# Turned operands in the mixer of a macaron decoder layer: rows of both blocks at once, p of two heads at once, k left as it lands

## The chip, the cores and the metric

One core of one Trainium2 chip runs the whole layer as one program. The metric is the device time of one execution in microseconds (us). Engines are named PE (TensorE matmul), PEld (its weight load), DVE (VectorE), ACT (ScalarE), POOL (GpSimd) and SP (SyncE, which here only issues DMAs).

## What is computed

256 tokens of width 2048 pass one decoder layer: a SwiGLU block, a token mixer of two branches, and a second SwiGLU block, each added to the scaled stream and normalised.

```python
h = layer_norm(ALPHA * h + 0.5 * swiglu(h, ffn1), ln1)          # d_ff 5632
c_q, c_kv, k_r, dq, dk, dv, gate_mla, gate_diff = split(h @ w_in)
q = rms_norm(c_q) @ w_uq                  # 8 heads of 128 + 64; the 64 are turned by rope
k_nope, v = rms_norm(c_kv) @ w_uk, rms_norm(c_kv) @ w_uv
o_mla  = softmax(q k^T, causal) v         # 8 heads
o_diff = (softmax(q1 k1^T + alibi) - lam * softmax(q2 k2^T + alibi)) dv   # 4 heads, rms-normed
y = sigmoid(gate_mla) * (o_mla @ w_branch_mla) + sigmoid(gate_diff) * (o_diff @ w_branch_diff)
h = layer_norm(ALPHA * h + y @ w_out, ln2)
h = layer_norm(ALPHA * h + 0.5 * swiglu(h, ffn2), ln3)
```

## The kernel before

All tokens stay on the chip as two row blocks b of 128 rows. Weights stream in from DRAM, 512 KB at a time. The large products keep fp32 accuracy with a split into a high and a low part: ACT casts a weight tile to the high part (L154), DVE takes the difference as the low part (L155), and three matmuls (hi x hi, hi x lo, lo x hi; lines L208, L209, L210) make one product. A unit of the schedule is one weight tile: its DMA, its cast and difference, and its matmuls, mostly 12.

**Order.** Each engine runs its own instructions in the order in which the program writes them. `unit` loads a tile, prepares it some units ahead of use in a ring of weight pairs (`wring`) and then writes its matmuls. `later(n, f)` writes f's instructions n units further on. So the side work of the mixer (softmaxes, transposed operands, gates) is strewn between the matmuls of the projections by the numbers given to `later`. `narrow_to(n)` sets how many pairs the ring has: six in the mixer. A pair takes two slots of the pool `act` (41 slots of 4 KB per partition). The pool `tmp` has six smaller slots, and products land in five PSUM banks (`mm`) and three (`tr`).

**Turning.** A matmul wants its activations with the model dimension on the partitions, so row blocks have to be transposed. Two ways are used. `rows_to_quad` transposes four 128x128 pieces with TensorE. `turn` goes through DRAM: DVE transposes a 128x512 row in squares of 32x32 into a tile "blocks" (`turn_out`, L715), POOL issues four writes of 64 KB (L717) into a DRAM tile "turn", some units later POOL issues the read of 256 KB into a tile "turned" (L729), and the user casts it (`turn_to_quad`, into the operands od, cn and y) or copies it into place (`turn_to_cols`, L737, for dqT, dkT, qT, qrT and kT). A quad is 512 of the model dimension. "blocks" and, for copies, "turned" lie in `tmp`. p of the softmax takes the same road in `turn_p`: one write "pturn" (L1107) and four reads "pt" (L1112).

**The mixer in time.** First come cn, ckv, the gates and the dq, dk, dv projections, then the four differential heads (scores L1237, values L1257 to L1259) between projections for the gates and for q, k and v of MLA; then the eight MLA heads (scores L1307 and L1309, values L1323 and L1324) between branch projections; then for f = 0 to 3 the product of om with the MLA branch, whose gated sum is y; then w_out on yq, whose quads f are turned as above. `v` is copied out of a bank at L1296, "junk" (L1263) is ACT's sum of squares of a differential head's output.

**h of the SwiGLU.** The product of gate and up is turned to DRAM (`hT`), and `get_h` (L895, POOL) reads a quad back as "hraw" when the down projection is near. The first three quads read are 3, 4 and 0, asked for 3, 6 and 9 units into the last group of gate and up; "sraw" and "raw" are weight tiles that SP loads meanwhile (L420, L457).

## Time and profile before

| | |
|---|---|
| median of 3 runs | 1989.48 us (1987.44 to 1990.28) |
| profiled execution | 1989.51 us, span 1987.7 us |
| granted TensorE clock | 0.995 of full speed |
| PE, DVE, ACT, POOL busy | 1956.0, 1782.5, 1239.5, 350.7 us |
| DMA | 494.61 MB, 249 GB/s |

Busy shares are averages over the whole span. A row of the waits view gives engine, line, the engine and line it waited for, the total, the count and the longest. A row of the stretches view gives the bounds, the length, the busy time of PE, PEld, DVE, ACT and POOL (with instruction counts), the granted clock, the busy share of the DMA engines and the GB/s. A row of the timeline gives start, duration, engine, line and operation, and in brackets the idle time ahead of it and what ended that. Groups give busy time and mean ns of one, then idle time before them. DMA rows give KB each and the median us from issue to landing.

### The profile page before, as it was taken

How to read it: one execution, taken by the hardware profiler on the slowest of the kernel's cores; microseconds unless marked ns; L12 is line 12 of the kernel's file. 1: busy time of each engine (PE TensorE's matmuls, PEld its weight loads, DVE VectorE, ACT ScalarE, POOL GpSimd, SP SyncE). 2: the span in 40 equal slices, each digit the busy share in tenths (PEclk: the TensorE clock that was granted, in tenths of full speed). 3: DMA queues.
4: the chain of work that ended last, by engine and by line, in shares of the span. 5: the costliest groups of instructions: out<-in, count | busy, mean ns of one | idle time of the engine just before them, and what ended most of it. 6: DMA issues, size and time to landing. Idle time of an engine off the chain costs nothing.

```text
span 1987.7 us, 25775 instructions
## 1 busy us (share of the span) xinstructions
PE 1956.0 (98%) x8716; PEld 1615.6 (81%) x8716; DVE 1782.5 (90%) x2191; ACT 1239.5 (62%) x1616; POOL 350.7 (18%) x603
## 2 busy tenths in 40 slices
PE   9999999999999999999998998999999999999997
PEld 7888888878888898888886786888888888788886
DVE  8999999998998879989986767789999999999986
ACT  6666666676665566666655654466666676665662
POOL 0112111222100010102246531001121112110000
PEclk9999999999999999999999999999999999999999
DMA  8978887878776666777677887779788878787763
GB/s 316 284 227 261 269 257 235 253 235 304 273 237 206 222 234 237 237 240 238 222 236 235 246 284 261 235 243 277 228 263 269 248 244 254 243 313 253 277 233 125
DMA packets 151444, 494.61 MB, mean 249 GB/s; under 512 B 22560, under 2 KB 22608, under 8 KB 151312
## 3 DMA queue, kind: packets, MB, share of 16 engines
q1 hardware_dynamic: 117360, 397.99, 58.1%
q0 software_dynamic: 33952, 94.98, 18.1%
q8 instruction: 68, 1.11, 0.2%
q14 instruction: 64, 0.52, 0.1%
HBM read 459.59 MB, written 33.29 MB: 248 GB/s over the span
## 4 chain that ended last, share of the span: by engine, by line
PE 86%; DMA 5%; DVE 4%; issue 2%; POOL 1%; ACT 1%; SPq 0%; DVEq 0%; POOLq 0%; ACTq 0%
PE mm L209 27%; PE mm L210 27%; PE mm L208 27%; DVE wring L155 2%; DMA turn<-blocks 1%; DMA turned<-turn 1%; DMA sraw<-in_gu_dram 1%; PE tr L209 1%; PE tr L210 1%; PE tr L208 1%; DVE sraw L428 1%; DMA pt<-pturn 1%; POOL turn L717 1%; ACT wring L154 1%; DMA gate<-gates 0%
## 5 line engine op out<-in xcount | busy, mean ns | idle before, releaser
L154 ACT CAST wring<-raw 128x1024 fp32r<-128x1024 f32 (+2 forms) x467 | 480.5, 1036 | 295.5 <-PE mm L210 196.4
L155 DVE TENSOR_TENSOR wring<-raw,wring 128x1024 fp32r<-128x1024 f32 (+2 forms) x467 | 556.9, 1202 | 85.4 <-ACT wring L154 83.6
L154 ACT CAST wring<-sraw 128x1024 fp32r<-128x1024 f32 x436 | 453.3, 1052 | 228.9 <-DVE sraw L428 95.0
L155 DVE TENSOR_TENSOR wring<-sraw,wring 128x1024 fp32r<-128x1024 f32 x436 | 521.2, 1222 | 19.4 <-ACT wring L154 16.5
L208 PE MATMUL mm<-wring,h 128*128 128x512 f32 (+2 forms) x1248 | 481.6, 386 | 2.3 <-ACT v L1296 2.3
L209 PE MATMUL mm<-wring,h 128*128 128x512 f32 (+2 forms) x1248 | 480.5, 385 | 0.2 <-DVE wring L155 0.2
L210 PE MATMUL mm<-wring,h 128*128 128x512 f32 (+2 forms) x1248 | 480.4, 385 | 0.0
L209 PE MATMUL mm<-wring,xs 128*128 128x512 f32 x776 | 302.3, 390 | 2.7 <-DVE wring L155 2.7
L208 PE MATMUL mm<-wring,xs 128*128 128x512 f32 x776 | 302.2, 389 | 0.0
L210 PE MATMUL mm<-wring,xs 128*128 128x512 f32 x776 | 302.0, 389 | 0.0
L208 PEld LDWEIGHTS mm<-wring,h 128*128 128x128 f32 x1248 | 234.7, 188 | 49.4 <-ACT v L1296 2.7
L209 PEld LDWEIGHTS mm<-wring,h 128*128 128x128 f32 x1248 | 234.8, 188 | 47.1 <-DVE wring L155 1.0
L210 PEld LDWEIGHTS mm<-wring,h 128*128 128x128 f32 x1248 | 234.8, 188 | 47.0 <-DVE h L155 0.7
L428 DVE TENSOR_TENSOR sraw<-sraw,sraw 128x1024 f32<-128x1024 f32 x168 | 199.4, 1221 | 3.7 <-DMA sraw<-in_wdv_dram 2.5
L209 PEld LDWEIGHTS mm<-wring,xs 128*128 128x128 f32 x776 | 145.7, 188 | 34.1 <-DVE wring L155 3.8
L208 PEld LDWEIGHTS mm<-wring,xs 128*128 128x128 f32 x776 | 145.6, 188 | 30.2
L210 PEld LDWEIGHTS mm<-wring,xs 128*128 128x128 f32 x776 | 145.7, 188 | 30.1
L717 POOL DMA_DIRECT2D hT<-blocks x176 | 96.9, 563 | 376.1 <-DVE blocks L715 373.7
L209 PE MATMUL mm<-wring,x 128*128 128x512 f32 x336 | 131.2, 390 | 1.0 <-DVE wring L155 0.9
L208 PE MATMUL mm<-wring,x 128*128 128x512 f32 x336 | 130.8, 390 | 0.0
L210 PE MATMUL mm<-wring,x 128*128 128x512 f32 x336 | 130.6, 389 | 0.0
L430 POOL DMA_DIRECT2D sraw<-in_gu_dram x40 | 35.4, 893 | 372.1 <-DVE sraw L428 368.9
(299 smaller groups left out, 2320.4 us busy)
## 6 DMA issues: line engine op xcount, KB each, us to landing
sraw<-in_gu_dram SPq DMA_DIRECT2D x160, 512.0 KB, 5.4
raw<-in_gu_dram SPq DMA_DIRECT2D x159, 512.0 KB, 4.9
raw<-in_dn_dram SPq DMA_DIRECT2D x140, 512.0 KB, 4.9
sraw<-in_gu_dram POOLq DMA_DIRECT2D x40, 512.0 KB, 7.1
sraw<-in_dn_dram SPq DMA_DIRECT2D x36, 512.0 KB, 5.9
hraw<-hT POOLq DMA_DIRECT2D x68, 256.0 KB, 6.5
eraw<-in_gu_dram SPq DMA_DIRECT2D x64, 256.0 KB, 5.8
raw<-in_w_out_dram SPq DMA_DIRECT2D x32, 512.0 KB, 5.2
```

The lines of the kernel that those rows point to most:

```text
L154: cast[0] = S.copy(hi, src)
L155: lows[0] = V.tensor_tensor(out=lo, in0=src, in1=hi.bitcast(F32), op=ALU.subtract)
L208: PE.matmul(o, xh, wh, start=first, stop=False, skip_group_check=again)
L209: PE.matmul(o, xh, wl, start=False, stop=False, skip_group_check=again)
L210: PE.matmul(o, xl, wh, start=False, stop=last, skip_group_check=again)
L428: last = V.tensor_tensor(out=R[src][i], in0=R[src][i], in1=R[add[1]][i], op=ALU.add)
L430: nc.gpsimd.dma_start(R["12"][s], source("22", s), accum_op=ALU.add)
L717: turned_out[0] = nc.gpsimd.dma_start(to.rearrange("(g r) (i f) -> i r g f", g=4, i=4)[i], t[32 * i:32 * (i + 1), :].rearrange("r (g f) -> ...
```

## The change

1. `turn_both` and `Cols`: the rows of both blocks share one "blocks" tile of 128x1024, four writes and one read of 512 KB. It serves qT, kT, qrT and the outputs of a pair of differential heads (od). dqT and dkT still leave row by row (`Cols.row`), but read back into one tile. All these tiles come from `act` rather than `tmp`.
2. k as the trip leaves it: dkT and kT are no longer copied into place; the score matmuls read them in runs of 32 columns (`keys`). Queries still are (`ordered`).
3. p of two MLA heads goes in one "pturn" of 128x768 and four reads "pt".
4. The ring has five pairs from the values projection of the differential heads to the end of the mixer, then six again.
5. y's last quad (f = 3) is transposed by TensorE (`rows_to_quad`); the last 512 rows of w_out are laid out to match. Quad 2's waits are (2, 3) units instead of (3, 3).
6. The first three quads of h are read by SP (`get_half`), one block at a time, at units 1, 3, 5, 7, 9 and 11.
7. Differential heads start one unit later; some other unit numbers change with the above.

```diff
+    def blocks_out(t, to):
+        for i in range(4):
+            nc.gpsimd.dma_start(to.rearrange("(g r) b (i f) -> i r b g f", g=4, i=4)[i],
+                                t[32 * i:32 * (i + 1)].rearrange("r b (g f) -> r b g f", g=4))
+
+    def turn_both(rows, use, wait, more):
+
+        t = act_tile([P, 2, 512], F32, "blocks")
+        V.transpose(t.rearrange("p b f -> p (b f)"), rows.rearrange("p b f -> p (b f)"))
+        to = dram.tile([P, 2, 512], F32, name=nm("turn"))
+        blocks_out(t, to)
+
+        def back():
+            t = act_tile([P, 2, 512], F32, "turned")
+            nc.gpsimd.dma_start(t, to)
+            for b in range(2):
+                later(more + b, lambda b=b: use(b, turned(t[:, b, :])))
+        later(wait, back)
+
+    class Cols:
+
+
+        def __init__(self, name, order=None):
+            self.name, self.order = name, order
+            self.t = None
+
+        def back(self, b, to):
+            if self.t is None:
+                self.t = act_tile([P, 2, 512], F32, self.name)
+                if self.order is not None:
+                    self.ordered = act_tile([P, 4, T], F32, self.name)
+            v = self.t if b is None else self.t[:, b, :]
+            nc.gpsimd.dma_start(v, to)
...
+        def row(self, row, b, wait):
+            to = dram.tile([P, 512], F32, name=nm("turn"))
+            turn_out(row, to)
+            later(wait, lambda: self.back(b, to))
+
+        def both(self, sources, wait):
+            t = act_tile([P, 2, 512], F32, "blocks")
+            for b, src in enumerate(sources):
+                V.transpose(t[:, b, :], src)
+            to = dram.tile([P, 2, 512], F32, name=nm("turn"))
+            blocks_out(t, to)
+            later(wait, lambda: self.back(None, to))
+
+        def at(self, k, b):
+            return self.ordered[:, k, b * P:(b + 1) * P]
+
+        def keys(self, k, n):
+            return self.t[:, 0:n].rearrange("p b (i k c) -> p k b i c", i=4, k=4)[:, k]
...
+        def get_half(q, b):
+            if b == 0:
+                got[q] = act_tile([P, 2, 512], F32, "hraw")
+            with tc.issue_after(fetched[0].ins):
+                nc.sync.dma_start(got[q][:, b, :], hT[q, b])
...
                 for i, q in enumerate((3, 4, 0)):
-                    later(3 + 3 * i, lambda q=q: get_h(q))
+                    for b in range(2):
+                        later(1 + 4 * i + 2 * b, lambda q=q, b=b: get_half(q, b))
...
+    def turn_p(ps, keep, more):
+
+        n = len(ps)
+        t = act_tile([P, n, 384], F32, "pblocks") if n > 1 else tmp_tile([P, 1, 384], "pblocks")
+        for i, p in enumerate(ps):
+            V.transpose(t[:, i, :], p)
+        to = dram.tile([P, n * 384], F32, name=nm("pturn"))
+        nc.gpsimd.dma_start(to, t.rearrange("p n f -> p (n f)"))
 
         def back():
-            pt = act_tile([P, 384], F32, "pt") if roomy else small.tile([P, 384], F32, tag="p", name=nm("pt"), bufs=3)
+            pt = act_tile([P, n, 384], F32, "pt") if n > 1 else small.tile([P, 1, 384], F32, tag="p", name=nm("pt"), bufs=3)
             for k in range(4):
-                nc.gpsimd.dma_start(pt[32 * k:32 * (k + 1), :].rearrange("f (b i c) -> f b i c", b=3, i=4),
-                                    to.rearrange("(i f) (b k c) -> k f b i c", i=4, b=3, k=4)[k])
-            keep["pt"] = pt
+                nc.gpsimd.dma_start(pt[32 * k:32 * (k + 1)].rearrange("f n (b i c) -> f (n b) i c", b=3, i=4),
+                                    to.rearrange("(i f) (b k c) -> k f b i c", i=4, b=3 * n, k=4)[k])
+            for i in range(n):
+                keep[i]["pt"] = pt[:, i, :]
         later(more, back)
...
+        def cols_proj(w, xx, kt, name, k0=0, order=None):
+            cols = Cols(name, order)
+            banks = []
 
             def done(b, bank):
-                later(1, lambda: turn_to_cols(bank, dst, b, 3, more))
+                banks.append(bank)
+                if b == 1:
+                    cols.both(banks, 3)
...
-        dqT = pair_cols(a["wdq"], "dqT")
+        dqT = pair_cols(a["wdq"], "dqT", 5)
         dkT = pair_cols(a["wdk"], "dkT")
...
+        narrow_to(5)
...
-                        PE.matmul(s[:, lo:hi], dqT[i // 4][:, i % 4, b * P:(b + 1) * P],
-                                  dkT[i // 4][:, i % 4, 0:hi - lo], start=True, stop=True)
...
-                    for b in range(2):
-                        later(2 + b, lambda b=b: turn_to_quad(rows[:, b, :], b, od, h // 2, 2, 3))
+                    later(1, lambda: turn_both(rows, lambda b, t: od.put(h // 2, b, t), 2, 2))
...
             for i, f in enumerate(diff_head(h)):
-                later(1 + 5 * h + (0, 3, 8)[i], f)
+                later(2 + 5 * h + (0, 3, 8)[i], f)
         gate(1, 2, c_back)
-        qT = [cols_proj(a["wuq"][c], cn, 4, "qT") for c in range(2)]
-        qrT = act_tile([P, 4, T], F32, "qrT")
+        qT = [cols_proj(a["wuq"][c], cn, 4, "qT", 0, 3) for c in range(2)]
+        qrT = Cols("qrT", 3)
+
+        qr_rows = act_tile([P, 2, 512], F32, "qr")
 
         def qr_done(b, bank):
-            t = tmp_tile([P, 512], "qr")
-            tv = t.rearrange("p (j h i) -> p j h i", j=2, h=MH)
+            tv = qr_rows[:, b, :].rearrange("p (j h i) -> p j h i", j=2, h=MH)
             rope(tv[:, 0], tv[:, 1], bank, b, MH)
-            later(1, lambda: turn_to_cols(t, qrT, b, 4, 5))
+            if b == 1:
+                qrT.both([qr_rows[:, n, :] for n in range(2)], 3)
         project(a["wuq"][2], cn, 4, 512, qr_done)
-        kT = [cols_proj(a["wuk"][c], cn, 4, "kT", 4, 4) for c in range(2)]
+        kT = [cols_proj(a["wuk"][c], cn, 4, "kT", 4) for c in range(2)]
...
+            def scores(n):
+                h = 2 * i + n
                 s = tr_bank()
                 for b, (lo, hi) in enumerate(SEG):
-                    n = hi - lo
-                    PE.matmul(s[:, lo:hi], qT[h // 4][:, h % 4, b * P:(b + 1) * P], kT[h // 4][:, h % 4, 0:n],
+                    PE.matmul(s[:, lo:hi], qT[h // 4].at(h % 4, b), kT[h // 4].keys(h % 4, b + 1),
                               start=True, stop=False)
-                    PE.matmul(s[:, lo:hi], qrT[:, h % 4, b * P:(b + 1) * P], krT[:, h // 4, 0:n],
+                    PE.matmul(s[:, lo:hi], qrT.at(h % 4, b), krT[:, h // 4, 0:hi - lo],
                               start=False, stop=True)
...
+                turn_p([t["p"] for t in st], st, 2)
...
+            return ((0, lambda: scores(0)), (1, lambda: scores(1)), (3, turn), (8, lambda: values(0)), (9, lambda: values(1)))
+
+        for i in range(MH // 2):
+            for n, f in mla_pair(i):
+                later(3 + 4 * i + n, f)
...
-                later(1, lambda: turn_to_quad(y[:, b, :], b, yq, f, *((4, 6) if f < 2 else (3, 3) if f == 2 else (1, 2))))
+                if f < 3:
+                    later(1, lambda: turn_to_quad(y[:, b, :], b, yq, f, *((4, 6) if f < 2 else (2, 3))))
+                else:
+                    later(2, lambda: rows_to_quad(y[:, b, :], b, yq, f))
...
+    narrow_to(6)
...
-    r["w_out"] = _chunks(_turned_rows(w["w_out"]), 512)
+    r["w_out"] = _chunks(np.concatenate([_turned_rows(w["w_out"][:1536]), w["w_out"][1536:]]), 512)
```

Where this moves instructions, in the order of each engine:

On DVE, after the softmax scores of the third differential head (`st`), before: the outputs of heads 0 and 1 (`orow`) are turned one row block at a time, with rows of kT's first product (`mm`) between.

```order
L715 STREAM_TRANSPOSE blocks_8308<-orow_8003 128x512
L155 TENSOR_TENSOR wring_115<-raw_8546,wring_114 128x1024
L715 STREAM_TRANSPOSE blocks_8320<-mm_8221 128x512
L1097 RECIPROCAL rs_8281<-sums_8278 128x2
L1088 TENSOR_REDUCE mx_8288<-st_8286 128x1
L1089 TENSOR_REDUCE mx_8288<-st_8286 128x1
L715 STREAM_TRANSPOSE blocks_8345<-orow_8003 128x512
L1091 TENSOR_SCALAR nmx_8291<-mx_8288 128x2
L1097 RECIPROCAL rs_8297<-sums_8294 128x2
L715 STREAM_TRANSPOSE blocks_8352<-mm_8260 128x512
L1242 TENSOR_SCALAR rl_8299<-rs_8297,lam 128x2
```

After, from the values of the second head on:

```order
L1149 TENSOR_REDUCE mx_8273<-st_8271 128x1
L1340 SCALAR_TENSOR_TENSOR orow_8009<-tr_8184,f_8206,subg 128x256 x2
L1150 TENSOR_REDUCE mx_8273<-st_8271 128x1
L744 STREAM_TRANSPOSE blocks_8236<-orow_8009 128x1024
L783 STREAM_TRANSPOSE blocks_8260<-mm_8157 128x512
L783 STREAM_TRANSPOSE blocks_8260<-mm_8227 128x512
L1152 TENSOR_SCALAR nmx_8276<-mx_8273 128x2
L1158 RECIPROCAL rs_8282<-sums_8279 128x2
L1149 TENSOR_REDUCE mx_8289<-st_8287 128x1
```

The two blocks of kT's first product (`blocks<-mm`) now stand next to each other, behind one 128x1024 transposition of both blocks of `orow`; the reductions of the second score tile and the weight difference that stood ahead of them now follow or lie earlier.

On POOL, from p of the third differential head (`pturn` of 128x384) to its reads, before:

```order
L1107 DMA pturn_8205<-pblocks_8203 128x384
L717 DMA turn_8209<-blocks_8210 32x4x128 x4
L729 DMA turned_8241<-turn_8119 128x512
L717 DMA turn_8243<-blocks_8244 32x4x128 x4
L729 DMA turned_8305<-turn_8146 128x512
L717 DMA turn_8307<-blocks_8308 32x4x128 x4
L1112 DMA pt_8314<-pturn_8205 32x12x32 x4
L717 DMA turn_8319<-blocks_8320 32x4x128 x4
```

After:

```order
L1170 DMA pturn_8212<-pblocks_8210 128x384
L768 DMA qT_8214<-turn_8122 128x1024
L738 DMA turn_8179<-blocks_8176 64x4x128 x4
L738 DMA turn_8238<-blocks_8236 64x4x128 x4
L738 DMA turn_8263<-blocks_8260 64x4x128 x4
L768 DMA qrT_8306<-turn_8179 128x1024
L1175 DMA pt_8309<-pturn_8212 32x12x32 x4
L750 DMA turned_8333<-turn_8238 128x1024
```

Between the write of that p and its four reads there stood three sets of four writes and two reads; now there stand one read, three sets of four writes of both row blocks (qr, od, kT) and the read of qrT. The read of the turned od follows it.

On ACT, where the MLA branch ends and w_out begins, before:

```order
L154 CAST wring_5085<-raw_9814 128x1024
L154 CAST wring_118<-raw_9834 128x1024
L154 CAST y_9725<-turned_9641 128x512
L154 CAST wring_116<-raw_9854 128x1024
L154 CAST y_9753<-turned_9662 128x512
L154 CAST y_9725<-turned_9695 128x512
L154 CAST wring_114<-raw_9873 128x1024
L154 CAST y_9753<-turned_9733 128x512
```

After:

```order
L154 CAST wring_102<-raw_9666 128x1024
L154 CAST wring_5085<-raw_9682 128x1024
L154 CAST wring_9557<-raw_9563 128x1024
L154 CAST y_9583<-turned_9514 128x512
L154 CAST y_9583<-tr_9587 128x512
L154 CAST y_9615<-turned_9536 128x512
L154 CAST wring_9557<-raw_9701 128x1024
L154 CAST y_9615<-tr_9623 128x512
L154 CAST wring_118<-raw_9721 128x1024
```

Of y's last two quads, both came by way of "turned"; now the last comes from `tr`, the PSUM bank of the TensorE transposition. `wring_9557` is the sixth pair that returns; its first cast stands behind the cast into `wring_5085`. On SP, the reads of h stand among the weight loads:

```order
L420 DMA sraw_463<-in_gu_dram 128x1024
L955 DMA hraw_3223<-hT_122 128x512
L457 DMA raw_3225<-in_gu_dram 128x1024
L955 DMA hraw_3223<-hT_122 128x512
L420 DMA sraw_466<-in_gu_dram 128x1024
L420 DMA sraw_467<-in_gu_dram 128x1024
L420 DMA sraw_460<-in_gu_dram 128x1024
L420 DMA sraw_461<-in_gu_dram 128x1024
L420 DMA sraw_464<-in_gu_dram 128x1024
L420 DMA sraw_465<-in_gu_dram 128x1024
L457 DMA raw_3270<-in_gu_dram 128x1024
L955 DMA hraw_3282<-hT_122 128x512 x2
```

They stood on POOL (`L895`), in one run of six, before.

58 lines of the change are left out of this document (25 added, 33 removed).

## Prediction

> **What bounds the kernel now.** I read the page first, then what TensorE waits for, then the stretches around those waits, then the instructions behind each. About 0.2% (4 us) is what a measurement of this kernel can tell from no change.
>
> ```profile
> PE 1956.0 (98%) x8716; PEld 1615.6 (81%) x8716; DVE 1782.5 (90%) x2191; ACT 1239.5 (62%) x1616; POOL 350.7 (18%) x603
> core 0: 1987.7 us, clock 0.995
> ```
>
> TensorE is busy for 1956.0 of 1987.7 us, so 31.7 us idle is nearly all that an edit of schedule can win. The waits say whose they are:
>
> ```profile
> PE mm L208 <- DVE blocks L715: 5.1, 2, 3.3
> PE mm L208 <- ACT y L154: 4.9, 3, 4.3
> PE mm L209 <- DVE wring L155: 3.8, 6, 1.7
> PE mm L208 <- ACT v L1296: 2.3, 1, 2.3
> PE mm L210 <- DVE y L155: 1.8, 1, 1.8
> PE tr L1323 <- issue: 0.6, 1, 0.6
> PE tr L1323 <- DMA pt<-pturn: 0.5, 2, 0.3
> PE mm L208 <- ACT od L154: 0.3, 1, 0.3
> ```
>
> These rows sum to 19.3 us; start and tail hold most of the rest and the change does not touch them. 15.5 us of the rows belong to the mixer, and 3.8 (weight pairs) mostly to the ends of the two gate/up passes. Two stretches hold the mixer's loss:
>
> ```profile
> 1030.00:1068.00 38.00, 30.55 (x123) 23.89 (x122) 28.99 (x63) 21.20 (x38) 27.19 (x49) 0.93 0.82 256
> 1195.00:1235.00 40.00, 33.36 (x131) 25.73 (x130) 26.51 (x34) 14.27 (x18) 8.75 (x16) 0.91 0.79 280
> ```
>
> I call them A (7.45 us idle, second column against first) and T (6.64 us). The granted clock is below 1 in both, and the timeline shows what that costs:
>
> ```profile
> 1048.46 0.51 PE L208 MATMUL mm<-wring,cn 128*128 128x512 f32 x1 [3.28 <-DVE blocks L715]
> 1050.05 0.63 PE L209 MATMUL mm<-wring,cn 128*128 128x512 f32 x1
> 1050.48 0.63 PE L210 MATMUL mm<-wring,cn 128*128 128x512 f32 x1
> 1052.44 0.40 PE L210 MATMUL mm<-wring,cn 128*128 128x512 f32 x1
> 1052.68 0.40 PE L208 MATMUL mm<-wring,cn 128*128 128x512 f32 x1
> 1217.00 0.79 PE L208 MATMUL mm<-wring,y 128*128 128x512 f32 x1 [4.25 <-ACT y L154]
> ```
>
> Behind the stall of 3.28 us the starts are 0.43 us apart, and from 1052.4 on 0.24: some 3.4 us at half speed, worth 1.7 us. The clocks of the two stretches, 0.07 x 38 and 0.09 x 40 us, make 2.7 and 3.6 us lost; I count two such windows, 3.4 us, in each (A's second is recorded behind the stretch). So A costs 10.9 us, T 10.0. The Trainium skill (TensorE: Matmul & The Clock Gate, HAM oscillation) puts the limit at idle gaps of over about 3.4 us; here 3.28 us sufficed, so the row decides.
>
> **Part by part.**
>
> *h's first quads in SP's queue.* At the end of each gate/up pass GpSimd issues six loads of h (L895) while SP issues four weight loads:
>
> ```profile
> 395.63 3.25 POOL L895 DMA_DIRECT2D hraw<-hT  x6
> 395.92 4.34 SPq L420 DMA_DIRECT2D sraw<-in_gu_dram  x4
> sraw<-in_gu_dram SPq DMA_DIRECT2D x160, 512.0 KB, 5.4
> ```
>
> 1.5 MB of h and 2 MB of weights share the engines for those 4 us, and TensorE then waits for a weight pair, up to 1.7 us (the row of 3.8 us above; some 1.9 us of it in ffn1 and 1.15 in ffn2). The change spreads the h loads over ticks 1 to 11, a unit of 12 matmuls (2.7 us) apart by twos, four of the six ahead of the four weight loads. The bytes are the same. SP's queue gets six more issues per pass, each for a buffer that has long been free, so nothing waits behind them. I take -2.8 of the 3.05; ends: -3.05, and +1, if loads behind them are late by as much as one issue each (4.34 / 4 = 1.1 us).
>
> *y's last quad by TensorE.* Block f = 3 of y no longer goes VectorE, GpSimd, DRAM, ScalarE. In T that trip ended late for both of its row blocks:
>
> ```profile
> 1203.86 0.71 DVE L715 STREAM_TRANSPOSE blocks<-diff 128x512 f32<-128x512 f32 x1
> 1216.33 0.62 ACT L154 CAST y<-turned 128x512 fp32r<-128x512 f32 x1 [8.36 <-DMA turned<-turn]
> L671 PE MATMUL tr<-ident,z 128*128 128x128 f32 x64 | 8.6, 277 | 0.3
> L154 ACT CAST wring<-raw 128x1024 fp32r<-128x1024 f32 x449 | 468.5, 1050 | 284.8 <-PE mm L210 192.0 <-DMA raw<-in_dn_dram 31.4 <-issue 21.1
> L155 DVE TENSOR_TENSOR wring<-raw,wring 128x1024 fp32r<-128x1024 f32 x449 | 543.7, 1221 | 79.0 <-ACT wring L154 77.4
> ```
>
> Eight transpositions are added to TensorE; at 8.6 / 64 that is 1.1 us, half of it inside the following stall. That stall is new: the sixth pair of the ring returns here, and its first cast stands on ScalarE behind a cast into the slot that the last matmul of om (time X) has just read. Two casts of 1.05 end at X + 2.1, VectorE's low halves at X + 2.3 and X + 3.5; the first matmul can go at X + 2.1, the second at X + 3.5. Stall about 3.1 us, with 0.5 of transposition inside, and half a slow window (0.9), since 3.28 brought one and 1.78 did not. After: 2.6 + 1.1 + 0.9 = 4.6; before 10.0. Quad 2 still makes the trip, but is needed only after four pairs on the first two quads, 10.9 us past the first matmul. I take -5.0; ends -6.4 (no stall from the casts beyond 2.1, no slow window) and 0, if quad 2's trip comes as late as quad 3's did here (its cast waited 8.36 us) and brings the old stall back.
>
> *Both rows turned together, p in pairs, k as it lands, five pairs: the middle of the mixer.* What is saved is queue time on GpSimd and buffers:
>
> ```profile
> 1052.49 6.72 POOL L717 DMA_DIRECT2D turn<-blocks  x12
> 1058.35 0.72 DVE L715 STREAM_TRANSPOSE blocks<-mm 128x512 f32<-128x512 f32 x1 [1.27 <-DMA turn<-blocks]
> ACT junk L1263 <- DMA turn<-blocks: 3.8, 1, 3.8
> L1112 POOL DMA_DIRECT2D pt<-pturn x48 | 32.0, 716 | 13.8 <-PE mm L210 5.4 <-DMA pturn<-pblocks 4.0 <-DMA turned<-turn 1.8
> turned<-turn POOLq DMA_DIRECT2D x34, 256.0 KB, 4.5
> ```
>
> An issue costs 0.56 to 0.72 us, whatever its size, and twelve in a row held the queue for 6.7 us. Then VectorE and ScalarE waited for "blocks" buffers of the six-slot pool, which made v late (2.31 us on TensorE). Each of qT, kT, qrT now issues 4 + 1 per pair of rows instead of 8 + 2, a pair of MLA heads 1 + 4 instead of 2 + 8, and the buffers come from the pool of 41. The stalls at 1059 and 1064 thus lose their cause.
>
> But in A the order sets up another. The transposition of kT's first block now waits for both rows, and holds two product banks meanwhile:
>
> ```profile
> 1035.09 1.47 PE L1237 MATMUL tr<-dkT,dqT 128*128 128x128 f32 x8
> 1042.57 0.83 DVE L1272 SCALAR_TENSOR_TENSOR orow<-tr,f,subg 128x256 f32<-128x256 f32 x2
> 1047.70 0.71 DVE L715 STREAM_TRANSPOSE blocks<-mm 128x512 f32<-128x512 f32 x1
> ```
>
> Count from the end of diff head 1's values (1035.1). VectorE's rows up to orow are the same ones, so orow ends at +8.3; then the double transposition (two of 0.71, with a reduction: +9.9) and kT's two, done at +10.6 and +11.3. By the order TensorE comes to need the bank after the scores (1.47) and some 16 matmuls (0.23 each), at +5.2: stall 5.4 us, against 3.28. Next, p of diff head 2: its four reads stand on GpSimd behind three sets of four writes and one read, 13 x 0.56 = 7.3 us after the double transposition is out, so issued up to about +18.2 and landed (3.6 to 4.5 us) at +22.2. TensorE has 12.1 us of work to there, so 22.2 - 12.1 = 10.1 us of idleness and slow clock together; 1.5 more for kT's second block, where before 18 matmuls (4.1 us) more stood ahead of head 2. Then one slow window of 1.7 that is not absorbed by the next wait, less the 0.9 by which these ends may overlap: 12.4 us against 10.9, **+1.5**. Ends: -7 if the writes land early and only the bank stall and one window are left, +5 if the 22.2 slips by another landing of 3.6.
>
> The output of a pair of diff heads now comes in one 512 KB read. The nearest rows are 256 KB at 4.5 us and SP's 512 KB at 5.4; issued about 12.8 us after the first MLA scores it lands at 18.3, and is cast one row at a time, against a need at 18.1: a stall of 1 to 2, where 0.3 stands. The MLA values wait for pairs: 1.1 us now, 1 to 2 then. Together **+1.6**, ends -1 and +4. The Trainium skill (DMA: Bandwidth & Descriptors, Anatomy of one DMA) gives 2.0 us + bytes / 436e3 for a GpSimd transfer, as an estimate 3.2 us for 512 KB; the sum would then be 1 us better. Its 2.6 us for 256 KB is under the 4.5 here, so I keep the rows.
>
> Eight copies of dkT and kT leave ScalarE, which waits anyway: nothing. The score matmuls read k in runs of 32 columns:
>
> ```profile
> 1102.03 0.39 PE L1307 MATMUL tr<-kT,qT 128*128 128x128 f32 x2
> 1102.25 0.39 PE L1309 MATMUL tr<-krT,qrT 128*128 128x128 f32 x2
> 1102.47 0.60 PE L1307 MATMUL tr<-kT,qT 128*128 128x256 f32 x2
> 1102.91 0.59 PE L1309 MATMUL tr<-krT,qrT 128*128 128x256 f32 x2
> ```
>
> No row shows such a read. One map takes 0.22 + 0.44 us of key matmuls, 16 maps 10.5: that is the upper end if they take twice as long; I take 0, since the count of columns is the same. The Trainium skill (SBUF — State Buffer, Terms) has a penalty only where an access leaves a 16-byte line; runs of 128 bytes would be free of it. No run here shows it. Five pairs instead of six let a cast start three slots of 2.7 us ahead of its use, 8.2 us, where cast and low half need 1.05 + 1.22: nothing.
>
> **Sum.** -2.8 - 5.0 + 1.5 + 1.6 = -4.7 us, on the profiled run's 1989.51 (span 1987.7 and 1.8 around it), which is the median of the runs (1989.48): **1984.8 us**.
>
> **Rivals.**
> 1. *The mixer's waits all go.* If buffers and GpSimd's queue were the only cause, A, T and the small waits shrink to the bank stall: 10.9 + 10.0 + 1.4 down to about 7, and h's 2.8: -18, 1971.5 us. For it: the wait of 3.8 us on "blocks". Against: the bank stall does not come from there. Chance, with what lies between it and the forecast's own range, 0.24.
> 2. *The new waits win (slower).* GpSimd's in-order queue: p of head 2 and the pair's read stand behind whole turns of two rows. If each lands one landing later than I count (3.6 us, at three places: head 2, od, the second MLA pair), with one more slow window, that is +10.8 + 1.7 over the forecast, less 3 that waits share: +9.5, so 1994.3. It decides where head 2's pt lands later than +24 after head 1's values. Chance 0.21.
> 3. *Strided keys.* Doubled: -4.7 + 10.5 = +5.8, 1995.3. Chance 0.05.
> 4. *Nothing to measure*: h's gain is real, T's is eaten by quad 2's trip and casts (0 in place of -5.0), the rest as summed: -2.8 + 1.5 + 1.6 = +0.3, 1989.8. Chance 0.10.
>
> **How the numbers follow.** The forecast has 0.40, with its own range 1980.5 to 1988.5; 0.28 of it lies past 0.2% (below 1985.5), 0.11 within, 0.01 beyond. Faster: 0.28 + 0.24 of the first rival = 0.52. Same: 0.11 + 0.09 of the fourth = 0.20. Slower: 0.21 + 0.05 + the last 0.02 = 0.28. The range leaves out about a tenth on each side: from 1974, inside the first rival, to 1996, past the second and third.
>
> **What would show it.** Right: no wait for wring at 417 and 1707; a stall of 2 to 3.5 us ahead of the first w_out matmul with casts behind it, and none for a turned y; the largest mixer stall at kT's bank, above 4 us, then one on pt of diff head 2. Wrong: no bank stall, or stalls on "turned" and pt of 3 us and more in the MLA heads, key matmuls longer than 0.39 and 0.60 us, or a wait for raw at the end of gate/up.

## The result, and the profile after

The changed kernel takes 1995.62 us (median of 7 runs, 1993.84 to 1996.56) against 1988.72 for the kernel before: a ratio of 1.0032, 95% interval 1.002 to 1.0044. That is 6.4 us slower by the ratio, where 4.7 us faster was forecast. The profiled execution's span is 1993.9 us (before: 1987.7).

The page's first part, after:

```profile
PE 1958.9 (98%) x8724; PEld 1621.4 (81%) x8724; DVE 1779.8 (89%) x2187; ACT 1238.2 (62%) x1608; POOL 312.0 (16%) x526
```

GpSimd issues for 312.0 us instead of 350.7, so the queue time that the change set out to save was saved. TensorE is no better off. Its waits in the changed kernel, of the whole span:

```profile
PE mm L208 <- DVE blocks L783: 7.4, 2, 5.7
PE mm L208 <- ACT wring L154: 4.6, 2, 3.7
PE mm L208 <- ACT od L154: 3.9, 1, 3.9
PE tr L1325 <- DMA pt<-pturn: 2.9, 1, 2.9
PE mm L209 <- DVE wring L155: 2.1, 5, 0.9
PE mm L208 <- ACT om L154: 1.2, 1, 1.2
```

Of the old waits, the one for `y` is gone, and so is `v` (2.3 us); within 380 to 430 and 1650 to 1720 us, where the end of gate and up had cost 1.9 and 1.1 us, no wait is left. In their place stand the banks of kT (L783), the second quad of od, p of the third differential head (L1325), a weight pair ahead of w_out, and om. The stretches of the mixer, with the same columns as before:

```profile
1030.00:1068.00 38.00, 27.65 (x106) 21.85 (x105) 24.54 (x55) 16.69 (x33) 17.03 (x29) 0.82 0.87 283
1068.00:1110.00 42.00, 38.09 (x167) 31.41 (x166) 29.13 (x64) 24.14 (x47) 12.05 (x18) 0.92 0.70 215
1110.00:1150.00 40.00, 40.00 (x192) 33.70 (x191) 22.84 (x53) 19.21 (x43) 13.45 (x20) 1.00 0.61 209
1150.00:1195.00 45.00, 42.35 (x180) 33.95 (x179) 32.85 (x42) 27.02 (x33) 16.92 (x30) 0.96 0.86 279
1195.00:1235.00 40.00, 36.07 (x150) 28.98 (x149) 29.52 (x37) 18.61 (x24) 6.61 (x12) 0.91 0.82 287
```

The granted clock is 0.82 and 0.92 in the first two stretches, where it was 0.93 and 0.98 before. To add up idle time and slow matmuls without counting twice, I take the starts of the weight matmuls (which cycle through L208, L209, L210, so a missing record can be told): whatever a start is later than 0.227 us after the one before, plus idle time ahead of the other matmuls. This "lost" time, by the program's sections, in us:

| section | before | after | difference |
|---|---|---|---|
| h, both SwiGLU blocks | 5.5 | 1.3 | -4.2 |
| q, k, v projections to the last differential head (A) | 11.5 | 14.2 | +2.7 |
| from there to od's last product | 3.6 | 8.8 | +5.2 |
| om | 0.1 | 5.2 | +5.1 |
| w_out (T) | 11.0 | 6.9 | -4.1 |
| the transpositions of y's last quad, added work | 0 | 1.2 | +1.2 |

The sum is +5.9 of the 6.2 us between the spans. A second profiled execution of the changed kernel (the run after_again below) gave 14.9, 10.1, 3.0 and 8.2 for the four mixer sections: the sum holds, single sections move by about 2 us, and a difference of that size between two traces decides nothing.

### The profile page after: what moved, and what is told of

The parts are those of the page before. It is cut to its first block, busy times and chain, and to the rows that moved or that the text cites. A ratio compares the mean times of both kernels' runs of the same rounds, so it can differ in the third digit from the quotient of the medians.

```text
span 1993.9 us, 25651 instructions
## 1 busy us (share of the span) xinstructions
PE 1958.9 (98%) x8724; PEld 1621.4 (81%) x8724; DVE 1779.8 (89%) x2187; ACT 1238.2 (62%) x1608; POOL 312.0 (16%) x526
## 4 chain that ended last, share of the span: by engine, by line
PE 92%; DMA 3%; DVE 2%; issue 1%; POOL 1%; ACT 1%; SPq 0%; DVEq 0%; ACTq 0%; POOLq 0%
PE mm L210 30%; PE mm L209 30%; PE mm L208 30%; DVE wring L155 1%; PE tr L210 1%; PE tr L209 1%; PE tr L208 1%; DMA raw<-in_w_out_dram 1%; PE tr L671 0%; DMA raw<-in_wbm_dram 0%; DMA turned<-turn 0%; DMA gate<-gates 0%; POOL turn L738 0%; DMA raw<-in_wuv_dram 0%; DMA raw<-in_gu_dram 0%
## 5 line engine op out<-in xcount | busy, mean ns | idle before, releaser
L208 PE MATMUL mm<-wring,h 128*128 128x512 f32 (+2 forms) x1248 | 480.7, 385 | 0.0
L210 PE MATMUL mm<-wring,h 128*128 128x512 f32 (+2 forms) x1248 | 479.8, 385 | 0.0
L209 PE MATMUL mm<-wring,h 128*128 128x512 f32 (+2 forms) x1248 | 479.8, 385 | 0.0
L209 PE MATMUL mm<-wring,xs 128*128 128x512 f32 x776 | 302.1, 389 | 0.4 <-DVE wring L155 0.4
L208 PE MATMUL mm<-wring,xs 128*128 128x512 f32 x776 | 302.2, 389 | 0.0
L210 PE MATMUL mm<-wring,xs 128*128 128x512 f32 x776 | 301.9, 389 | 0.0
L208 PEld LDWEIGHTS mm<-wring,h 128*128 128x128 f32 x1248 | 234.6, 188 | 46.6 <-ACT h L154 0.6
L209 PEld LDWEIGHTS mm<-wring,h 128*128 128x128 f32 x1248 | 234.4, 188 | 46.6 <-DVE wring L155 0.4
L210 PEld LDWEIGHTS mm<-wring,h 128*128 128x128 f32 x1248 | 234.4, 188 | 46.5 <-DVE h L155 0.7
L209 PEld LDWEIGHTS mm<-wring,xs 128*128 128x128 f32 x776 | 145.7, 188 | 31.0 <-DVE wring L155 1.0
L210 PEld LDWEIGHTS mm<-wring,xs 128*128 128x128 f32 x776 | 145.7, 188 | 30.2
L208 PEld LDWEIGHTS mm<-wring,xs 128*128 128x128 f32 x776 | 145.7, 188 | 30.1
L208 PE MATMUL mm<-wring,x 128*128 128x512 f32 x336 | 130.8, 390 | 0.9 <-ACT wring L154 0.9
L209 PE MATMUL mm<-wring,x 128*128 128x512 f32 x336 | 131.0, 390 | 0.6 <-DVE wring L155 0.6
L210 PE MATMUL mm<-wring,x 128*128 128x512 f32 x336 | 130.6, 389 | 0.0
```

Of the source, the lines that this page charges most:

```text
L208: PE.matmul(o, xh, wh, start=first, stop=False, skip_group_check=again)
L209: PE.matmul(o, xh, wl, start=False, stop=False, skip_group_check=again)
L210: PE.matmul(o, xl, wh, start=False, stop=last, skip_group_check=again)
```

## The experiments

All ratios are to the kernel before, which ran in the same group of runs on the same chip; the groups ran on three chips, with 5 to 12 executions of each run's kernel. Single executions of one kernel differ by up to 0.65% (1979.71 to 1992.57 us for the run with q and k by rows), and each trace is one of them. Where a gain below is given against the changed kernel, it is the difference of two ratios, the changed kernel's being 1.0032 in its first group and 1.0036 in the second. That second value is as expected (1.0015 to 1.005). The "larger pool" is `act`, from which the changed kernel takes the tiles of the turns.

| run | what it is | ratio, 95% interval |
|---|---|---|
| after_again | the changed kernel once more | 1.0036, 1.0023 to 1.0049 |
| h_only | before + h by SP | 0.9976, 0.9966 to 0.9986 |
| y_only | before + y's last quad by TensorE | 0.9983, 0.9974 to 0.9991 |
| hy_late | before + both, transpositions later | 0.9965, 0.9951 to 0.9978 |
| b_ring5 | before + five pairs | 1.0003, 0.9994 to 1.0012 |
| a_cols_rows | after, q and k by rows | 0.9979, 0.9967 to 0.9991 |
| a_od_rows | after, od by rows | 0.9991, 0.9983 to 0.9999 |
| a_p_single | after, p of one head at a time | 1.0022, 1.0012 to 1.0032 |
| a_all_rows | after, the three together | 0.9990, 0.9980 to 1.0001 |
| a_rows_od | after, q, k and od by rows, p in pairs | 0.9966, 0.9954 to 0.9978 |
| a_ring6 | after, six pairs throughout | 0.9998, 0.9989 to 1.0007 |
| a_ring5long | after, five pairs through w_out | 1.0010, 1.0001 to 1.0020 |
| a_y_late | after, transpositions later | 1.0035, 1.0021 to 1.0048 |
| best1 | a_all_rows, six pairs, late | 0.9957, 0.9941 to 0.9973 |
| best2 | a_rows_od, six pairs, late | 0.9927, 0.9913 to 0.9941 |
| best2_kcopy | best2, k copied into place | 0.9938, 0.9924 to 0.9952 |

**h alone.**

```diff
...
-                    later(3 + 3 * i, lambda q=q: get_h(q))
+                    for b in range(2):
+                        later(1 + 4 * i + 2 * b, lambda q=q, b=b: get_half(q, b))
```

> The kernel before with one part alone: the first three quads of h are read by SP, one block at a time. Theory S (the change is a sum of parts, each paid where its stall stands): the waits for weight pairs at the end of gate and up go, with the slow matmuls behind them, 2.5 + 1.7 us in the traces of before and after, so -3 to -4.2 us, about 1985. Rival R (that gain also needs the other parts, because GpSimd's queue is shorter in them): under 1 us.

0.9976, 4.8 us, as theory S has it and a little more. The gain needs no other part.

**y's last quad alone.**

```diff
+                if f < 3:
+                    later(1, lambda: turn_to_quad(y[:, b, :], b, yq, f, *((4, 6) if f < 2 else (3, 3))))
+                else:
+                    later(2, lambda: rows_to_quad(y[:, b, :], b, yq, f))
...
```

> The kernel before with one part alone: y's last quad by TensorE, w_out laid out to match; six pairs throughout. Theory S: T lost 10.8 us in before (idle and slow matmuls); here no pair returns at that place, so what is left is the transpositions (1.1) and up to 2 us for quad 2: -7 to -9 us, about 1981. Rival R (the weight load for the first w_out products comes late by itself, so the stall of 3.7 us appears here too): -3 us, as in the changed kernel.

0.9983, 3.4 us: the size that rival R gave, but not by its mechanism. The waits of this run between 1040 and 1235 us hold no weight pair. TensorE now waits for VectorE's sum of y, since the transpositions stand ahead of w_out's first matmuls in its order (a row of that view):

```profile
PE tr L671 <- DVE diff L1360: 3.3, 1, 3.3
```

**od by rows.**

```diff
-                    later(1, lambda: turn_both(rows, lambda b, t: od.put(h // 2, b, t), 2, 2))
+                    for b in range(2):
+                        later(2 + b, lambda b=b: turn_to_quad(rows[:, b, :], b, od, h // 2, 2, 3))
```

> The changed kernel with the output of a pair of differential heads turned row by row again (64 KB writes, 256 KB reads, each row cast as it lands). Theory S: the stall of 3.9 us ahead of the first product on od's second quad, and the slow matmuls behind it, 6.8 us together, shrink to about 1: -4 to -6 us against the changed kernel, about 1990. Rival R (od is late because the last differential head ends late, whatever the size of its turn): within 1.5 us of it.

0.9991 against 1.0032 and 1.0036: 8 to 9 us, more than expected. The lost time between the last differential head and od's end falls from 8.8 to 3.4 us, and the wait for od halves; the 3 us or so beyond that have no place in this trace. The row for od, of the waits of this run:

```profile
PE mm L208 <- ACT od L154: 1.9, 1, 1.9
```

**p of one head at a time.**

```diff
...
-            return ((0, lambda: scores(0)), (1, lambda: scores(1)), (3, turn), (8, lambda: values(0)), (9, lambda: values(1)))
+            return ((0, lambda: scores(0)), (2, lambda: turn_one(0)), (2, lambda: scores(1)), (4, lambda: turn_one(1)), (6, lambda: values(0)), (8, lambda: values(1)))
```

> The changed kernel with p of the MLA heads turned one head at a time, at the unit numbers of before. Theory S: pairing p let the gate reads bunch ahead of the last pair's reads, ScalarE waited for a gate, the weight loads behind it came late, and TensorE lost 5.7 us between 1110 and 1190 against 2.2 in before: -3 us, about 1992.5. Rival R (the loss there comes from five pairs in place of six): within 1 us of the changed kernel, with the same waits for wring and om.

1.0022, 2 to 3 us less than the changed kernel; the two intervals overlap. In the trace om's loss is gone (0.2 us), but A and T have grown by 2 each. Not decided by this run.

**h and y, transpositions five units after the sum.** The two edits above, with one line of the second changed:

```diff
-                    later(2, lambda: rows_to_quad(y[:, b, :], b, yq, f))
+                    later(5, lambda: rows_to_quad(y[:, b, :], b, yq, f))
```

> The kernel before with two parts: h's first quads by SP, and y's last quad by TensorE, its transpositions asked for five units after the sum instead of two, so that w_out's first products stand ahead of them. In the run with y's part alone TensorE waited 3.28 us in front of the transpositions, for VectorE's sum. Theory S (parts add up): -4.8 for h, -3.4 for y, and -3 to -4 for that wait: -9 to -12 us against before, about 1979. Rival R (w_out's first weights come too late to use the place, so the wait moves to a weight pair): -6 to -8.

0.9965, 7.0 us by the ratio, which is in rival R's range; the medians differ by 9.3, which is in theory S's. The interval, 4 to 10 us, takes in both: not decided. What rival R gave as its reason isn't seen, since no weight pair is waited for at w_out. The wait for the sum is gone too. What remains at w_out is 2.5 us of waiting for y's last quad: its cast out of PSUM (`y<-tr`) stands on ScalarE behind the cast of the quad before, which waited for its read, and behind three weight casts (ScalarE's timeline of this run):

```profile
1206.75 0.62 ACT L154 CAST y<-turned 128x512 fp32r<-128x512 f32 x1 [9.57 <-DMA turned<-turn]
1207.28 2.94 ACT L154 CAST wring<-raw 128x1024 fp32r<-128x1024 f32 x3
1210.13 0.57 ACT L154 CAST y<-tr 128x512 fp32r<-128x512 f32 x1
```

**q and k by rows.**

```diff
-                banks.append(bank)
-                if b == 1:
-                    cols.both(banks, 3)
+                later(1, lambda: cols.row(bank, b, 3))
```

> The changed kernel with q's and k's projections turned row by row (each row's four writes of 64 KB and read of 256 KB, as soon as its product is done); the rope part of q still goes both at once. Theory S: the product bank of kT's first row is no longer held for the second row, so the stall of 5.67 us falls to the 3.3 of before: -2 to -4 us against the changed kernel, about 1992. Rival Q (the bank waits for VectorE's queue, where both heads' outputs, the rope sums and weight differences stand ahead anyway; the extra eight issues delay the reads of p): within 1.5 us of it, or slower.

0.9979, 11 us under the changed kernel: three times the expected. The profiled execution took 1989.86 us, 5.6 above this run's median, so its trace locates only a part of the gain. Its waits in the mixer, the six largest:

```profile
PE mm L208 <- ACT wring L154: 3.1, 1, 3.1
PE mm L208 <- ACT v L1363: 3.0, 1, 3.0
PE mm L208 <- ACT om L154: 3.0, 1, 3.0
PE mm L208 <- ACT od L154: 2.5, 1, 2.5
PE tr L671 <- DVE diff L1428: 2.5, 1, 2.5
PE tr L1323 <- DMA pt<-pturn: 2.2, 1, 2.2
```

No wait for a bank is left (7.4 us in the changed kernel), although VectorE has the same transpositions to do. So turning both rows of q and k at once was the cause of the stall, and rival Q falls. Theory S expected the 3.3 us of before to remain, and they are gone too, here and in every later run that turns these rows singly. VectorE's order may be why: three of the four transpositions of kT's rows now stand ahead of the outputs of the second differential head, where all stood behind them in the changed kernel and in the one before (VectorE's timeline of this run, the first such row and the head's outputs):

```profile
1036.92 0.70 DVE L715 STREAM_TRANSPOSE blocks<-mm 128x512 f32<-128x512 f32 x1
1041.49 0.87 DVE L1338 SCALAR_TENSOR_TENSOR orow<-tr,f,subg 128x256 f32<-128x256 f32 x2
```

How much is due to the bank held for the second row, and how much to this place in the order, the run doesn't separate. A loses 8.5 us, less than the 11.5 of before. The loss at od fell too (8.8 to 4.9) with od's turn untouched: part of it seems to be the earlier stall's, handed on, but GpSimd's queue ahead of od's turn changed as well, and no run separates the two.

**Six pairs, and five pairs for longer.** In the first, `narrow_to(5)` is left out, in the second `narrow_to(6)` behind the mixer.

> The changed kernel with six weight pairs throughout (two slots of the pool fewer for tiles). Theory S: the middle of the mixer stays as it is, and only the stall of 3.70 us ahead of w_out goes with the returning pair, but VectorE's sum of y then stands there, as with y's part alone: 0 to -2 us against the changed kernel. Rival R (five pairs are what makes casts late in the MLA heads and before w_out): -5 us or more. A third: slots for tiles run short and reads of turned rows start late: slower by 3 or more.

> The changed kernel with five pairs through w_out too, so that no new pair returns there. If the returning pair's place behind the cast of the last om weights makes the stall of 3.70 us ahead of w_out: -2 to -4 us against the changed kernel. If the stall is the late load of weights or VectorE's sum for the transpositions, it stays: within 1 us of it.

0.9998 and 1.0010: 7 and 4 to 5 us under the changed kernel. The first is the size that rival R gave, the second a little more than was expected of the returning pair; the two differ by 2.4 us, and their intervals overlap. In the traces T falls from 6.9 and 8.2 to 3.6 and 5.2, and the wait of 3.4 to 3.7 us for a weight pair ahead of w_out is gone in the first (the second has three of 1.2 us and less, later on). The rest is not seen at one place: the profiled execution of the run with six pairs was the slowest of its eleven (1994.66 us).

**Five pairs alone.** The kernel before with `narrow_to(5)` and `narrow_to(6)` added.

> The kernel before with one part alone: five pairs from the values projection of the differential heads to the end of the mixer, then six. Theory F (five pairs cost by themselves: later casts, and the returning pair's first cast stands behind another ahead of w_out): +4 to +7 us against before. Theory N (they cost only together with y's transpositions, which stand in the same place): within 1.5 us of before.

1.0003. Ahead of w_out the returning pair costs a stall as large as in the changed kernel (this run's waits, one row):

```profile
PE mm L208 <- ACT wring L154: 4.5, 1, 4.5
```

That is theory N. The stall costs nothing there because w_out would have waited for y's last quad anyway: the waits for y are 0.6 us in this trace and were 6.7 in the kernel before, and T loses 8.4 us against 11.0. With y's quad made early, nothing covers the stall.

**Transpositions later in the changed kernel.** The same edit as above, `later(5, ...)`.

> The changed kernel with y's last transpositions asked for five units after the sum instead of two; five pairs and the returning sixth stay. If the transpositions' place makes the loss ahead of w_out (they wait for VectorE's sum, 1.6 to 5 us in the traces of this group): -3 to -5 us against the changed kernel, about 1991. If the returning pair's cast makes it (3.1 to 4.4 us in every trace that has it): within 1.5 us of it.

1.0035, no change. It doesn't tell the two apart: in TensorE's order only the second block's transpositions moved, the first four kept their place ahead of w_out, and its trace has both waits, 4.1 us for VectorE's sum and 4.2 for the weight pair.

**The three groupings undone, and all but p.** These are the edits above together.

> The changed kernel with all three groupings undone: q's and k's projections row by row, od row by row, p one head at a time (k as it lands, the larger pool, five pairs, h by SP and y's last quad stay). Theory G (the three groupings are the loss, each at its own place: 5.7 us at kT's banks, 5.4 at od, 5.0 at om, from the single undoings): -10 to -16 us against the changed kernel, 1980 to 1986. Rival R (five pairs are the loss, the groupings only shift it): no better than the best single undoing, 1985 to 1990.

> As the kernel with all three groupings undone, but p still in pairs. Theory G: om keeps its 5 us, the other two places are gone: 4 to 5 us slower than that kernel. Rival P (pairs of p cost nothing net: alone, their undoing gained 2 us or less, since single heads wait for their own reads): within 2 us of it.

0.9990 and 0.9966: theory G falls in both. The first is where rival R had it; the second goes the other way by 4.8 us, beyond the 2 us of rival P. With p single and the rest undone, A loses 6.2 us and om 0.2, but the MLA heads wait for their own reads and the loss moves to them and to T (9.2 and 11.5). The first three waits in the mixer of the run with all three undone:

```profile
PE tr L1395 <- DMA pt<-pturn: 5.9, 2, 4.7
PE tr L671 <- DVE diff L1432: 5.0, 1, 5.0
PE mm L208 <- ACT wring L154: 4.0, 1, 4.0
```

Left in pairs, p costs 2.8 us in om and saves 4.3 before it, and T loses less too: pairs are a gain of 4.8 us by the ratios, with intervals that don't overlap, not a loss.

**The best version, and what k as it lands is worth.** `best1` is the kernel with all three undone, six pairs and late transpositions; `best2` the same with p in pairs; `best2_kcopy` copies dkT and kT into place again:

```diff
...
-            return self.t[:, 0:n].rearrange("p b (i k c) -> p k b i c", i=4, k=4)[:, k]
+            return self.ordered[:, k, 0:n * P]
...
```

> All three groupings undone, six pairs throughout, and y's last transpositions asked for five units after the sum: what is left of the change is h by SP, y's last quad, k as it lands and the larger pool. If the parts add: A as in the run with rows (8.5 us lost), od and om as in before (3 to 4), T as in the late variant (5): 1976 to 1980, under both kernels and under the run with h and late y (0.9965). Rival: k as it lands and the larger pool bring nothing by themselves: 1980 to 1983, the same as that run.

> q's, k's and od's turns row by row, p in pairs, six pairs of weights, y's last transpositions five units after the sum. If the sections add as the traces have them (5.5 us lost to the last differential head, 4.9 to od's end, 2.8 in om, 1.5 at w_out): 3 to 4 us under the run with single p and six pairs, about 1976. Rival: pairs of p only helped while five weight pairs made casts late: the same as that run, 1980.

> As best2, with dkT and kT copied into place again (eight copies of 0.62 us on ScalarE, contiguous keys). If k as it lands is free and copies hide: within 1 us of best2. If the copies stand ahead of v's copy or the softmaxes on ScalarE: 1 to 4 us slower. If reading in runs cost TensorE time: faster, which the equal durations of the key matmuls (380 and 380 ns) speak against.

`best1` has 0.9957, 8.6 us under before and 1981.9 us by the ratio: the rival's range, with an interval that takes in the run with h and late y (0.9965). `best2` takes 1975.19 us, where about 1976 was expected, ratio 0.9927: 14.5 us under the kernel before and some 21 under the changed one. It is 6 us under `best1`, with intervals that just touch, so pairs of p seem to help with six weight pairs too; the rival, no difference, falls by the measured values. Its page and its waits in the mixer:

```profile
PE 1950.6 (99%) x8724; PEld 1616.4 (82%) x8724; DVE 1779.8 (90%) x2189; ACT 1237.4 (63%) x1608; POOL 326.5 (17%) x556
```

```profile
PE mm L208 <- ACT v L1363: 2.9, 1, 2.9
PE tr L1391 <- DMA pt<-pturn: 1.7, 2, 1.0
PE mm L208 <- ACT om L154: 1.2, 1, 1.2
PE mm L210 <- DVE y L155: 1.0, 1, 1.0
PE mm L208 <- ACT y L154: 0.9, 1, 0.9
PE mm L210 <- DVE om L155: 0.3, 1, 0.3
```

The largest wait left is 2.9 us for v. Copying k again is 2 us worse by the ratio and 3 by the medians, with intervals that overlap: between free and slightly worse it is not decided. What the larger pool, the heads one unit later and the shorter waits of quad 2 are worth was not run by itself.

## Why the prediction was wrong, step by step

**What failed** is the step "Together +1.6" for the second quad of od and the pairs of MLA heads, with ends -1 and +4, and with it the forecast's sum. It measured +5.2 and +5.1 (+6.5 and +2.9 in the second execution). Of the 10.6 us between the forecast's -4.7 and the table's +5.9 this step is 8.7, T 2.1 and A 1.2, and h gives 1.4 back. The step priced the landing of od's read too low, left out the slow matmuls behind its stalls, which the prediction counted in A and T, and expected the loss of the pairs at p's reads, where there is none. One of the prediction's own signs of being wrong came: a stall of over 3 us behind "turned", 3.9 at od.

The read of od was put at some 5.5 us, after SP's 512 KB row. But GpSimd, which issues it, had a row of that size in the kernel before, and it says 7.1 us (the first line below, of that kernel's DMA view). The second quad's two reads of 256 KB, too, took 6.5 and 6.6 us before, where the forecast had the 4.5 that is the median over the whole kernel. In the changed kernel od's reads are the slowest of the 512 KB turns (6.1 us for qT, 5.6 for kT); the view of their line, L750:

```profile
sraw<-in_gu_dram POOLq DMA_DIRECT2D x40, 512.0 KB, 7.1
```

```profile
L750 POOL DMA_DIRECT2D turned<-turn x2: 542/665/788, 1056.5 to 1096.1; - x2
  ACT od L154: 4.1, 1
DMA to landing us min/median/max: 6.9/7.4/7.9
```

The second quad's read took the longer of these, 7.9 us. The prediction's estimate from the Trainium skill (DMA: Bandwidth & Descriptors, Anatomy of one DMA), 3.2 us, is further off: the measurement decides. Count, as the forecast did, from the first MLA scores (1082.33). The read was to be issued at +12.8, to land at +18.3, and to be needed at +18.1; it was issued at +13.7 (1096.07), landed at +21.7 (1104.0), and was needed at +18.4. The issue came 5.9 us after that of the last of the four writes (1090.17). 4.2 of these were that write's own landing; in the rest, a store of gates and p of the MLA heads stood ahead in GpSimd's order and had waited for their data (1093.52 and 1095.14). In the kernel before, counted from its own first scores (1079.74), the two rows came at +17.4 and +21.7. So the second row came no later than before; the first came 4 us later, since it shared the read. The stall was 3.9 us instead of 1 to 2, and TensorE ran at half speed behind it (its timeline, after):

```profile
1104.67 0.80 PE L208 MATMUL mm<-wring,od 128*128 128x512 f32 x1 [3.91 <-ACT od L154]
1105.27 0.63 PE L209 MATMUL mm<-wring,od 128*128 128x512 f32 x1
1105.69 0.63 PE L208 MATMUL mm<-wring,od 128*128 128x512 f32 x1
```

For the pairs of MLA heads the forecast had 1 to 2 us of waiting for p's reads. The changed kernel has no such wait; the loss is in om. There ScalarE waited for gates, as its timeline in the changed kernel shows:

```profile
1149.24 1.28 ACT L1425 ACT_TABLE_LOAD   x1 [3.73 <-DMA gate<-gates]
```

Casts, and so weight loads, stood behind it: SP issued none between 1144.57 and 1155.52, and the next four landed after 7 to 9 us beside the next eight reads of gates. That the pairs of p let the gates' reads stand together was my reading of the trace, and not shown: undoing the pairs alone gained 2 to 3 us at most, with overlapping intervals, and with the other groupings undone the pairs were a gain.

**A's bank stall was right**: 5.4 and 1.5 us were forecast for kT's two blocks, and 5.67 and 1.77 measured. p of head 2 was to land at +22.2 after head 1's values and landed at +23.8, with a wait of 2.92 us. +2.7 was lost where +1.5 stood (TensorE's timeline, after, at kT's bank):

```profile
1048.89 0.79 PE L208 MATMUL mm<-wring,cn 128*128 128x512 f32 x1 [5.67 <-DVE blocks L783]
```

That the joined rows of q and k cause it was shown by the run that undoes them. What a sum of places can't have is that the loss at od fell with it, as told there.

**T** gained 2.9 us net (-4.1 and 1.2 of transpositions) where 5.0 stood. The stall in front of w_out came where it was forecast, 3.70 us for 3.1, with the returning pair's cast behind another cast. That the sizes are so close is in part luck: the forecast let the other cast wait for om's last matmul (1205.41), but it waited beyond that for its weights, which took 6.1 us to land (ScalarE's timeline, after; both casts are in this line):

```profile
1207.89 1.99 ACT L154 CAST wring<-raw 128x1024 fp32r<-128x1024 f32 x2 [2.36 <-DMA raw<-in_w_out_dram]
```

Quad 2 was in time. Not seen ahead: VectorE's sum of y stands in front of the transpositions, with no other work of TensorE between. It cost nothing in this execution, 1.6 us in the second one, and up to 5 in other runs.

**h** gained 4.2 us, outside my ends (-3.05): I had counted the idle time alone, without the slow matmuls behind it.

**Five pairs at "nothing"**: the prediction charged the returning pair in T, with 3.1 us, and put nothing for the rest. Added to the kernel before, they are free (1.0003). In the changed kernel six pairs were worth 7 us by the ratio, and five pairs that never return to six 4 to 5. So most of the price seems to be the returning pair's, which w_out waits for once y's quad is made early; whether five pairs cost anything earlier in the mixer stays open.

**k as it lands at 0** was right; the reads in runs of 32 columns take no longer than contiguous ones (380 ns in the kernel before too), so the third rival falls. The rule of the Trainium skill that the prediction names there (SBUF — State Buffer) stands on that page under Specifications (TRN2), not under Terms, and asks for two hits in each 16-byte line; runs of 128 bytes hit each line as often as contiguous rows do. The equal durations agree (groups of the changed kernel):

```profile
L1376 PE MATMUL tr<-kT,qT 128*128 128x256 f32 x16 | 4.8, 380 | 0.0
L1305 PE MATMUL tr<-dkT,dqT 128*128 128x256 f32 x16 | 4.8, 380 | 0.0
```

The second rival came nearest: new waits for what stands behind whole turns in GpSimd's queue, 1994.3 us, with 0.21. Its mechanism is borne out at od alone, which came 3.4 us later than counted, about the one landing that it gave. Its test place, p of head 2, stayed just short of +24, and at the MLA pairs no read was waited for. That its total fits as well as it does is therefore in part luck.

As to the clock, the stalls of 5.67 and 3.91 us were followed by matmul starts 0.43 us apart, where 0.23 is usual. In `best2`, where no other stall is near, 2.92 us brought the same for 3.4 us. The Trainium skill (TensorE: Matmul & The Clock Gate, HAM oscillation) warns of idle gaps of over about 3.4 us; a shorter one was enough here. The timeline of `best2`:

```profile
1062.72 0.50 PE L208 MATMUL mm<-wring,h 128*128 128x512 f32 x1 [2.92 <-ACT v L1363]
...
1065.54 0.63 PE L209 MATMUL mm<-wring,h 128*128 128x512 f32 x1
1065.96 0.63 PE L210 MATMUL mm<-wring,h 128*128 128x512 f32 x1
...
1066.70 0.40 PE L209 MATMUL mm<-wring,h 128*128 128x512 f32 x1
1066.94 0.40 PE L210 MATMUL mm<-wring,h 128*128 128x512 f32 x1
```

What stays open: why six pairs are worth 7 us when T accounts for 3 to 4; how the groupings' losses hang together, since undone singly they gain 11, 8 to 9 and 2 to 3 us, and all three together only 9; and whether the groupings of q and k could be kept with more banks, which was not tried.

## What to carry to other kernels

Joining two transfers saves issue time on a queue that may not be the bound, and it makes the first half wait for the second: ask what the first half holds meanwhile (here a product bank) and who needs it alone. Price a new stall with the slow matmuls behind it, and a read by rows of its own queue and size and by the landing times at its own place. Parts of one change do not add: p in pairs did nothing measurable while the other groupings stood, and was a gain of 5 us without them, so undo parts in company before judging them.

## What the hardware showed unexpectedly

Reading the moving operand in runs of 32 columns (128 bytes), four runs per 128 columns, cost nothing: 380 ns for 256 columns either way. VectorE's transposition of 128x1024 took 1.24 us, where two of 128x512 took 1.37 (686 ns each):

```profile
L783 DVE STREAM_TRANSPOSE blocks<-mm 128x512 f32<-128x512 f32 x8 | 5.2, 686 | 0.0
L744 DVE STREAM_TRANSPOSE blocks<-orow 128x1024 f32<-128x1024 f32 x2 | 2.5, 1236 | 0.0
```
